# S5 outputs and the norm of k get a place in TensorE's order: a hybrid S5 / DeltaNet / mixture-of-experts layer on one core

## The chip, the cores and the metric

The kernel runs on one NeuronCore of a Trainium2 chip. The time is that of one execution on the device in microseconds (us). Each of the engines TensorE (PE; its weight loads are PEld), VectorE (DVE), ScalarE (ACT), GpSimd (POOL) and SyncE (SP) works through its own list of instructions in order; they wait for each other by semaphores. SP and ScalarE also issue the transfers (DMA); "SPq" and "ACTq" mark such issues.

## The reference, cut to what matters

One layer with 256 latent tokens behind 256 context tokens, width 1024, all in float32.

```python
h  = rmsnorm(x,   norm1) * (1 + sc1)  + sh1        # modulation from silu(c) @ w_mod
hc = rmsnorm(ctx, norm1) * (1 + csc1) + csh1
u, qkv, gate, b, a, br = split(h @ w_in)           # 512, 1536, 512, 8, 8, 2048 columns; the same for hc
qkv = silu(short_conv(qkv))                        # 5 taps along the tokens
# branch A: S5, 32 groups of 16 channels, 64 complex states, two directions
y = d*u + sum over directions of readout(complex_scan(A, B u), C)   # the scan starts from the context's end
ya = z * sigmoid(z @ w_glu + b_glu),  z = gelu(y)
# branch B: gated DeltaNet, 4 heads of 128, chunks of 64, two directions
q = l2norm(q) * 128**-0.5 ;  k = l2norm(k)         # l2norm(t) = t * rsqrt(sum(t*t) + eps)
# per chunk: a triangular solve on k k^T, then a scan over the 8 chunks with a 128 x 128 state
yb = rmsnorm(o) * norm * silu(gate)
ga, gb = sigmoid(br)
x = x + gt1 * ((ga * (ya @ w_branch_a) + gb * (yb @ w_branch_b)) @ w_out)
# mixture of experts: top 4 of 32, w_gate_up 1024 x 2048 and w_down 1024 x 1024 for each, 403 MB in all
out = rmsnorm(x + gt2 * moe(rmsnorm(x, norm2) * (1 + sc2) + sh2), norm_f)
```

## The kernel before

`front` does everything up to DeltaNet's scan over the chunks, `merge` the output projection, `moe` the experts. The experts' weights are streamed once by SP, a tile of 1 MB at a time, into every register that the front part has given back.

The front part is a list of small steps, written out in `ORDER` (line 187) and traced in that order by the loop in `front`. `u`, `k`, `v`, `q`, `gate` and `br` are blocks of 128 columns of the input projection (4, 4, 4, 4, 4 and 16 of them). The first three kinds (`proj_cm`) cover all 512 tokens with 8 matmuls, which the trace shows as 16 instructions `ps<-h,win`. The last three (`proj_lat`) cover the latent tokens only: ScalarE and VectorE split the block's weights into a high and a low half (`wsp`), and TensorE runs 16 instructions `ps<-hx,wsp`. `k`, `v` and `q` go on to the short convolution on VectorE and ScalarE (`conv`: `raw`, `cacc`, `cth`). `mod` is one piece of the modulation of the second half (`ps<-wm,sc`, 1 MB of `w_mod` each). Tiles `win`, `wsp` and `wm` share five buffers of 1 MB.

- `l2k` (line 729, through `l2`, line 693) norms k: ScalarE squares it (`sq`), TensorE sums the squares (`ps<-ones,sq`), VectorE and GpSimd take the root (`rnk`), TensorE spreads it, VectorE multiplies k. `gdn_a` (line 1044) then forms the chunks' matrices, passes them through DRAM (`ad`, `M`) and solves them on VectorE (`fst`, `Y`).
- `s5_in0/1`, `s5_scan` (VectorE) and `s5_steps` (GpSimd, 31 steps on `XL`) are the S5 scan in blocks of 8 tokens.
- `s5_K` (line 490) builds the kernel within a block (`ps<-R,BB` on TensorE, then `KS` on ScalarE and VectorE). `s5_T` (line 558) copies it by 32 transfers of 64 KB into `T`, 16 issued by ScalarE and 16 by SP.
- `s5_out` (line 887) makes S5's output: 64 instructions `ps<-T,U`, then 256 `ps<-R,XL`, then the gelu into `z`.
- `gdn_b0` and `gdn_b1` prepare DeltaNet's scan; they write into registers that `s5_out` reads. `br@3000` are branch-gate blocks with a lower priority, which fill TensorE.

The order of the list is not yet the order on an engine. A planner simulates the program when it is built and lets each engine take, among the instructions whose inputs it believes ready, the one with the best priority; SP alone keeps the written order. A matmul's priority is that of its step (`rank`). `tc.issue_after(ins)` adds an edge to the planner: what the block traces on `ins`'s engine is placed behind `ins` in that engine's order, with no wait for its end. `self.last` is the matmul traced last.

Of the kernel before, what the change touches and what calls it, by code (L numbers as in the profile page):

```python
# [27 lines left out]
class Kern:  # L28
# [114 lines left out]
    def front(self):  # L143
        tc, nc = self.tc, self.nc
        self.smalls()
        self.load_x()
        self.s5_load(0)
        self.mod1()
        self.s5_load(1)
        self.wins, self.winq, self.pair = self.win_order(), [], {}  # L150
        self.ba_load()
        for _ in range(self.WIN0):
            self.win_load()
        self.load_h()
        self.mod1_end()
        self.modulate()
        self.s5_prep()
        self.CC, self.R = [[self.raw[:, i, :16] for i in (2, 3)], None], {}
        self.P = [None, self.s5_P(1)]
        self.P[0] = self.s5_P(0)  # L160
        self.s5_R0()
        self.s5_C()
        step = dict(
            k=self.proj_k(), u=self.proj_u(), v=self.proj_v(), q=self.proj_q(), gate=self.gate(),
            mod=self.mod2(), br=self.br(), ba=self.branch_a())
        for x in self.ORDER.split():
            n, _, times = x.partition("*")
            n, _, pr = n.partition("@")
            for _ in range(int(times or 1)):
                p0 = tc.cur_priority  # L170
                if pr:
                    tc.cur_priority = p0 + int(pr)
                self.rank = tc.cur_priority
                if n in step:
                    next(step[n])()
                else:
                    getattr(self, n)()
                if pr:
                    tc.cur_priority = p0
        self.rank = None  # L180
        assert not any([list(x) for x in step.values()])
        self.gdn_scan()
        tc.cur_priority += 5000
        self.merge()

    ENG_P, ENG_R, ENG_E = "VVVVVGVV", "GGGGGGGG", "VVVV"
    ORDER = """proj_ba u*5 mod*2 gdn_e k mod k s5_in0 s5_in1 mod k mod k s5_scan s5_R1 mod v l2k gdn_a s5_steps
        mod v mod v mod v mod s5_K lat q mod q s5_T mod q mod q mod l2q mod*2 gate*4 br*2 s5_out gdn_b0
        br@3000*14 gdn_b1 s5_glu@500 ba@500*8"""

    def mod1(self):
        nc, I, wk = self.nc, self.I, self.wk
# [386 lines left out]
    def win_order(self):  # L579

        left = {n: iter([c + x // 2 if x % 2 == 0 else None for x in range(b)]) for n, (c, b) in self.W_IN.items()}
        for x in self.ORDER.split():
            n, _, times = x.partition("*")
# [1205 lines left out]
```

## Time and profile before

| | us |
|---|---|
| median of 3 runs (1449.15 to 1454.15) | 1453.27 |
| the profiled execution | 1453.78 |
| its span, first to last instruction | 1452.1 |
| TensorE busy | 1338.0 (92%) |
| VectorE busy | 559.1 (39%) |
| ScalarE busy | 255.4 (18%) |
| GpSimd busy | 179.1 (12%) |

The shares are means over stages with different limits: in the first 200 us VectorE is busy most of the time, from 240 to 470 us TensorE is, and from about 545 us on the transfers run at some 410 to 420 GB/s without a break.

### The profile page before, as it was taken

To read this page: it belongs to the slowest core of one execution; us is meant where nothing else is said; L and a number is where in the kernel's file an instruction comes from. 1 tells how busy PE (TensorE), PEld (TensorE's weight loads), DVE (VectorE), ACT (ScalarE), POOL (GpSimd) and SP (SyncE) were. 2 spreads that over 40 slices of the span, in tenths; PEclk is the share of its full clock that TensorE was granted. 3 is DMA by queue.
4 is the path that set the end of the run, shared out by engine and by line. 5 is a ranking of instruction groups with operands and counts; after the bars stand their busy time and mean duration, and the time that the engine had idled before them with its cause. 6 is when DMAs were issued, how large, how long until landed. Compare 5 with 4: busy or idle time off the path is not lost. (4 is left out here: it accounts for less than half of the span.)

```text
span 1452.1 us, 18531 instructions
## 1 busy us (share of the span) xinstructions
PE 1338.0 (92%) x7469; PEld 600.9 (41%) x7469; DVE 559.1 (39%) x1083; ACT 255.4 (18%) x568; POOL 179.1 (12%) x299
## 2 busy tenths in 40 slices
PE   4799784999999899999999999999999999999985
PEld 1244362768787533333333333333333333333321
DVE  4977977664254403222322322232222222222213
ACT  3224321524301111011110110111011101111001
POOL 1921875111000100000000000000000000000000
PEclk9799896999999899999999999999999999999998
DMA  9464236711638899999999999999999999999994
GB/s 341 193 139 146 88 77 178 223 59 59 197 123 329 281 356 416 419 419 420 419 418 419 420 418 419 419 420 418 419 420 419 418 420 419 419 419 419 419 420 188
DMA packets 93275, 473.06 MB, mean 326 GB/s; under 512 B 24912, under 2 KB 29160, under 8 KB 41344
## 3 DMA queue, kind: packets, MB, share of 16 engines
q1 hardware_dynamic: 73216, 461.08, 79.4%
q10 hardware_dynamic: 19968, 10.73, 3.5%
q8 instruction: 61, 1.00, 0.3%
q14 instruction: 30, 0.25, 0.1%
HBM read 466.52 MB, written 3.16 MB: 323 GB/s over the span
## 5 line engine op out<-in xcount | busy, mean ns | idle before, releaser
L79 PE MATMUL ps<-w,xT 128*64 128x512 f32 x2048 | 485.7, 601 | 9.0 <-DMA w<-in_w_gate_up_dram 8.8
L79 PEld LDWEIGHTS ps<-w,xT 128*64 128x64 f32 x2048 | 137.6, 137 | 272.6 <-issue 241.8
L79 PE MATMUL ps<-w,aT 128*64 128x512 f32 x1024 | 233.1, 597 | 11.4 <-DMA w<-in_w_down_dram 11.1
L1725 DVE SCALAR_TENSOR_TENSOR od<-ps,cs,gt 128x512 f32<-128x512 f32 x31 | 23.3, 750 | 468.7 <-PE ps L79 468.7
L79 PEld LDWEIGHTS ps<-w,aT 128*64 128x64 f32 x1024 | 71.6, 137 | 165.5 <-issue 126.4
L94 DVE TENSOR_TENSOR x<-x,ps 128x512 f32<-128x512 f32 x128 | 84.1, 684 | 66.4 <-PE ps L79 66.4
L1506 POOL CAST selsd<-biad 128x128 fp32r<-128x128 f32 x32 | 9.4, 294 | 703.5 <-PE ps L79 703.5
L97 ACT ACTIVATE odh<-od 128x512 fp32r<-128x512 f32 x31 | 19.5, 629 | 427.0 <-DVE od L1725 427.0
L79 PE MATMUL ps<-h,win 128*128 128x512 f32 x192 | 91.3, 616 | 0.0
L79 PE MATMUL ps<-hx,wsp 128*128 128x256 f32 (+1 forms) x384 | 81.8, 360 | 0.0
L79 PEld LDWEIGHTS ps<-hx,wsp 128*128 128x128 f32 x384 | 62.9, 198 | 20.1 <-issue 9.8
L79 PE MATMUL ps<-h,oh 128*64 128x512 f32 x248 | 63.0, 604 | 0.0
L79 PEld LDWEIGHTS ps<-h,win 128*128 128x128 f32 x192 | 35.0, 195 | 47.6 <-issue 45.8
L97 ACT ACTIVATE sgm<-gt 128x512 f32<-128x512 f32 (+1 forms) x33 | 20.3, 618 | 163.6 <-DVE gt L1696 163.6
L79 PE MATMUL ps<-wm,sc 128*32 128x512 f32 x192 | 29.3, 699 | 20.2 <-DMA wm<-in_w_mod_dram 20.2
L97 ACT ACTIVATE aT<-ps 128x512 f32<-128x512 f32 (+1 forms) x33 | 19.3, 584 | 141.9 <-PE ps L83 141.9
L1696 DVE TENSOR_SCALAR gt<-ps 128x512 f32<-128x512 f32 (+1 forms) x33 | 22.2, 675 | 57.1 <-PE ps L79 57.1
L94 DVE TENSOR_TENSOR wsp<-win,wsp 128x512 fp32r<-128x512 f32 x48 | 32.0, 701 | 23.8 <-ACT wsp L97 23.5
L685 DVE SCALAR_TENSOR_TENSOR cacc<-raw,col_gdn_conv,cacc 128x512 f32<-128x512 f32 (+1 forms) x48 | 36.3, 756 | 5.5 <-ACT cacc L97 5.3
L1506 POOL CAST selsg<-biad 128x256 fp32r<-128x256 f32 x32 | 13.7, 427 | 190.7 <-PE ps L79 184.5
L97 ACT ACTIVATE wsp<-win 128x512 fp32r<-128x512 f32 x48 | 27.5, 624 | 49.2 <-PE ps L79 27.0
L79 PE MATMUL ps<-bias,selsg 128*128 128x512 f32 x64 | 28.6, 472 | 7.1 <-DVE ut L1698 6.6
(367 smaller groups left out, 1465.9 us busy)
## 6 DMA issues: line engine op xcount, KB each, us to landing
w<-in_w_gate_up_dram SPq DMA_DIRECT2D x242, 1024.0 KB
w<-in_w_down_dram SPq DMA_DIRECT2D x121, 1024.0 KB
wm<-in_w_mod_dram SPq DMA_DIRECT2D x24, 1024.0 KB
win<-in_w_in_dram SPq DMA_DIRECT2D x18, 1024.0 KB
w<-in_w_gate_up_dram SPq DMA_DIRECT2D x28, 512.0 KB
w<-in_w_down_dram SPq DMA_DIRECT2D x14, 512.0 KB
wo<-in_w_out_dram SPq DMA_DIRECT2D x4, 1024.0 KB
wa<-in_w_branch_a_dram SPq DMA_DIRECT2D x4, 512.0 KB
```

What stands on the lines that cost most here:

```text
L79: self.last = self.nc.tensor.matmul(out, lhsT, rhs, start=start, stop=stop, **kw)
L94: (eng or self.nc.vector).tensor_tensor(out, a, b, op=op)
L97: self.nc.scalar.activation(out, in_, func, **kw)
L685: nc.vector.scalar_tensor_tensor(acc[:, rows], rt[:, rows, k:k + 64], sc, acc[:, rows], op0=OP.mult, op1=OP.add)
L1506: nc.gpsimd.tensor_copy(v.rearrange("p (n s) -> p n s", s=CAP), dup[:, x:x + n, None].to_broadcast([128, n, CAP]))
L1696: V.tensor_scalar(g, z0, 7.0, None, op0=OP.min)
L1725: V.scalar_tensor_tensor(od, self.pd, self.cs, k.gt2, op0=OP.mult, op1=OP.mult)
```

## The change

`s5_out` and `l2k` are traced inside `issue_after` of the last matmul traced before them. `l2k`, with `gdn_a` and `s5_steps` behind it, moves in the list from behind the first v block to behind the second. One of the fourteen low-priority branch-gate blocks becomes a third normal one, ahead of `s5_out`.

```diff
                 if n in step:
                     next(step[n])()
+                elif n in self.BEHIND:
+
+                    with tc.issue_after(self.last.ins):
+                        getattr(self, n)()
                 else:
                     getattr(self, n)()
...
+    BEHIND = ("l2k", "s5_out")
     ENG_P, ENG_R, ENG_E = "VVVVVGVV", "GGGGGGGG", "VVVV"
-    ORDER = """proj_ba u*5 mod*2 gdn_e k mod k s5_in0 s5_in1 mod k mod k s5_scan s5_R1 mod v l2k gdn_a s5_steps
-        mod v mod v mod v mod s5_K lat q mod q s5_T mod q mod q mod l2q mod*2 gate*4 br*2 s5_out gdn_b0
-        br@3000*14 gdn_b1 s5_glu@500 ba@500*8"""
+    ORDER = """proj_ba u*5 mod*2 gdn_e k mod k s5_in0 s5_in1 mod k mod k s5_scan s5_R1 mod v mod v l2k gdn_a s5_steps
+        mod v mod v mod s5_K lat q mod q s5_T mod q mod q mod l2q mod*2 gate*4 br*3 s5_out gdn_b0
+        br@3000*13 gdn_b1 s5_glu@500 ba@500*8"""
```

## Rows read from the trace of the kernel before

**Rows 1.** Stages: start:end, length, busy us (instructions) by engine, TensorE's clock, DMA share, GB/s.
```profile
145.00:182.00 37.00, 28.81 (x207) 14.36 (x200) 36.73 (x43) 12.16 (x35) 31.97 (x27) 0.86 0.26 86
...
236.00:240.00 4.00, 0.00 (x0) 0.00 (x0) 0.00 (x0) 0.00 (x0) 3.52 (x12) 0.50 0.47 107
...
330.00:400.00 70.00, 69.93 (x661) 57.67 (x660) 25.56 (x48) 29.52 (x70) 4.70 (x5) 0.98 0.43 137
...
545.00:1452.00 907.00, 864.75 (x3933) 302.25 (x3929) 232.24 (x413) 104.71 (x223) 21.51 (x60) 0.99 0.99 410
```

**Rows 2.** TensorE's waits up to 520 us: waiter, awaited, us in total, times, longest.
```profile
PE ps L79 <- DMA T<-KS: 25.0, 3, 15.2
...
PE ps L79 <- ACT sq L97: 8.2, 1, 8.2
```

**Rows 3.** Timeline of TensorE: start, us, instruction, count, idle time before and its end.
```profile
143.73 1.13 PE L79 MATMUL ps<-h,win 128*128 128x512 f32 x2
...
162.32 1.87 PE L79 MATMUL ps<-ones,sq 128*128 128x1 f32 x8 [8.19 <-ACT sq L97]
164.05 2.06 PE L79 MATMUL ps<-h,win 128*128 128x512 f32 x2
```

**Rows 4.** Timeline of ScalarE: v's convolution, then KS.
```profile
161.12 0.63 ACT L97 ACTIVATE cth<-cacc 128x512 f32<-128x512 f32 x1 [14.74 <-DVE cacc L685]
...
207.05 0.60 ACT L97 ACTIVATE KS<-ps 128x512 f32<-128x512 f32 x1 [8.11 <-PE ps L79]
...
208.04 0.55 ACT L97 ACTIVATE KS<-ps 128x448 f32<-128x448 f32 x1 [0.39 <-DVE KS L94]
```

**Rows 5.** Timeline of VectorE around KS.
```profile
199.43 0.21 DVE L94 TENSOR_TENSOR KS<-KS,ps 128x64 f32<-128x64 f32 x1
200.52 1.28 DVE L94 TENSOR_TENSOR A<-A,ps 128x512 f32<-128x512 f32 x2 [0.88 <-PE ps L79]
...
207.68 0.35 DVE L94 TENSOR_TENSOR KS<-KS,dd 128x64 f32<-128x64 f32 x1
208.61 0.22 DVE L94 TENSOR_TENSOR KS<-KS,ps 128x64 f32<-128x64 f32 x1 [0.58 <-ACT KS L97]
```

**Rows 6.** Timeline of SP: its half of the transfers of T.
```profile
208.86 15.93 SPq L564 DMA_DIRECT2D T<-KS  x16
```

**Rows 7.** Timeline of TensorE around q's second and third block.
```profile
210.43 3.07 PE L79 MATMUL ps<-hx,wsp 128*128 128x512 f32 x16
...
240.53 1.03 PE L79 MATMUL ps<-T,U 128*32 128x128 f32 x4 [15.17 <-DMA T<-KS]
241.49 5.40 PE L79 MATMUL ps<-hx,wsp 128*128 128x512 f32 x16
...
247.73 1.07 PE L79 MATMUL ps<-T,U 128*32 128x128 f32 x24
```

**Rows 8.** Timeline of ScalarE: issues of T, then weight splits.
```profile
224.41 16.28 ACTq L564 DMA_DIRECT2D T<-KS  x8
240.74 0.63 ACT L97 ACTIVATE wsp<-win 128x512 fp32r<-128x512 f32 x1 [15.93 <-DMA T<-KS]
...
256.61 0.64 ACT L97 ACTIVATE wsp<-win 128x512 fp32r<-128x512 f32 x1 [1.02 <-PE ps L79]
```

**Rows 9.** Timeline of VectorE: the split for q's third block.
```profile
241.40 0.69 DVE L94 TENSOR_TENSOR wsp<-win,wsp 128x512 fp32r<-128x512 f32 x1 [6.65 <-ACT wsp L97]
```

**Rows 10.** One stage, as rows 1: instructions on XL alone, then on T (PE, PEld).
```profile
241.00:285.00 44.00, 6.21 (x119) 4.51 (x119) 0.00 (x0) 0.00 (x0) 0.00 (x0) 0.94 0.67 203
...
241.00:285.00 44.00, 3.33 (x55) 2.18 (x53) 0.94 0.67 203
```

**Rows 11.** Timeline of TensorE ahead of the first gate.
```profile
254.66 0.88 PE L79 MATMUL ps<-R,XL 64*32 64x128 f32 x18
...
256.47 1.74 PE L79 MATMUL ps<-R,XL 64*32 64x128 f32 x50
```

**Rows 12.** Timeline of GpSimd: the last scan step.
```profile
239.20 0.71 POOL L94 TENSOR_TENSOR XL<-XL,scu 128x64 f32<-128x64 f32 x2
```

**Rows 13.** Waits of SP's queue from 100 to 600 us, as rows 2: weights of the experts.
```profile
SPq L1420 <- PE ps L79: 119.8, 37, 14.5
```

## Prediction

> **What bounds the kernel now.** I read the stages first. From 545 us on the transfers are busy 0.99 of the time and TensorE 864.75 of 907 us, so the mixture of experts is worth nothing to this change except through the moment at which it begins. Between 330 and 400 us TensorE is busy 69.93 of 70 us: whatever TensorE gains or loses before that comes out again behind it. Between 145 and 182 us it is VectorE that is full, 36.73 of 37 us, while TensorE has gaps [rows 1]. The list of TensorE's waits then gives those gaps their names: 25.0 us for the transfers of T out of KS, in three pieces, and 8.2 us in one piece for the squares of k on ScalarE [rows 2]. These two are what the change is aimed at, 33.2 us together. Whether the time behind them goes depends on what the next instruction in TensorE's order would have been waiting for at that moment, so I read the same two stretches on the other engines.
>
> **The norm of k.** TensorE has reached the first sum of squares at 154.1 us and gets its input at 162.32; one matmul of the second v block (two of its sixteen instructions) stands behind it in order [rows 3]. The input is late because ScalarE, in its order, waited 14.74 us for VectorE's convolution of v before it came to the square [rows 4]. With the norm behind the second v block TensorE goes on: that last matmul, the weights of the modulation, the third v block. So 8.2 us of TensorE's time come free, and a little more, since the two v instructions behind the gap took 2.06 us where the same two took 1.13 before it [rows 3]: at most 9.1. Below it is bounded by 0, if the sums of squares again stand in front of something and wait for ScalarE.
>
> What the gain is worth is decided by the next common point, KS. The transfers of T start at 208.86 us [rows 6], right behind the last step of KS on VectorE, which follows two copies on ScalarE (0.60 and 0.55 us); the first of these waited 8.11 us for the matmuls of KS [rows 4]. So TensorE sets KS, and 8.2 us would go through, but VectorE is without a gap until 199.64 (199.43 + 0.21) [rows 5]. From there 0.60 + 0.55 on ScalarE and 0.35 + 0.22 on VectorE give 201.36 as the earliest start of T [rows 4, 5]: 208.86 - 201.36 = 7.5. I take **-7.5**, because the row of KS names TensorE and VectorE is no nearer than that; the bounds are -9.1 and 0.
>
> With the norm two more steps move back by one v block. The 31 scan steps on GpSimd end at 239.92 (239.20 + 0.71) [rows 12], and their first reader, the S5 output, now stands far behind: nothing. The solve of DeltaNet's blocks (with its transfers on ScalarE's queue, which are the same in number) runs on VectorE in the long gap before q's third block, where VectorE sat idle for 6.65 us [rows 9]. A v block is sixteen instructions, 8 x 1.13 = 9.0 us [rows 3]; if the solve moves by all of it, 9.0 - 6.65 = 2.4 us land on the splits of the weights. Bounds 0 and +2.4; I take 0, since KS moves forward while the solve moves back.
>
> **The S5 output, the long wait.** TensorE ends q's second block at 213.50 (210.43 + 3.07), and in the trace the next entries in its order are four instructions on T, three times, the last at 240.53; q's third block starts at 241.49 [rows 7]. The change takes these twelve instructions out. What is next then is q's third block, and it needs weights that ScalarE and VectorE split. ScalarE does that split at 240.74, after 15.93 us idle: it stood there issuing the last eight of its sixteen transfers of T, from 224.41 to 240.69 [rows 8]. These issues keep their place, because the step that makes T stands ahead of q's third block in the written order, and nothing in the change touches that. So TensorE waits until 241.49 as before, with another name in the list of waits. I take **0**; the bounds are 0 and -16.3 (rival B).
>
> The twelve instructions ran in time that was lost anyway. Later they cost 12 x 1.07 / 24 = **+0.5** [rows 7].
>
> Then the rest. From 241 to 285 us the S5 output is spread between the blocks of q, the gates and two branch gates: 6.21 us of the scan part and 3.33 us of the T part [rows 10]. All of it now runs in one piece behind the third branch-gate block, the work being the same. It costs nothing where the next block was ready and was only held up; where the block was not ready, the matmuls covered a wait that is now bare. Bounds 0 and +9.5. The clearest covered wait is ahead of the first gate: two groups of 0.88 and 1.74 us stand there [rows 11], and ScalarE's split for that gate came late, at 256.61, after waiting for TensorE to give a buffer back [rows 8]. I take these two, **+2.6**, because the other blocks show no such wait on ScalarE.
>
> Moving one branch-gate block ahead of the S5 output adds no instruction and no transfer, and the order of the SP queue stays the same, since neither moved step issues anything on it. The steps behind the S5 output get their registers about a block later, while TensorE has thirteen branch-gate blocks to fill with: 0.
>
> **The sum.** -7.5 + 0 + 0.5 + 2.6 = -4.4 us. It is passed on whole: TensorE is full up to 400 us [rows 1], and the loads of the experts' weights wait for TensorE 119.8 us in 37 waits [rows 13], so they start earlier by as much. The profiled execution took 1453.78 us (span 1452.1 and 1.7 around it): 1449.4. The median of the runs is 0.5 lower, so **1449**.
>
> **The rivals.** Case A is this forecast, own range 1443 to 1455.
>
> B: the T wait is really shortened. If the weights of q's third block are split before ScalarE's last eight issues, TensorE can start 0.75 us (241.49 - 240.74) behind 224.41 instead of at 241.49, which is 16.3 us more [rows 7, 8]: 1449 - 16.3 = 1433. For it: the trace names nothing but the issues as what held ScalarE. Against it: the written order puts T first. The Trainium skill (DMA: Bandwidth & Descriptors, "Issuing engines are not separate DMA queues") says that the time a sequencer needs to start a transfer is usually small beside the transfer; by it ScalarE would be through with T at once and this case would be the likeliest. The trace disagrees: eight issues held ScalarE 16.28 us [rows 8].
>
> C: the change does not do what it says; both waits come back under another name, the first as a wait for the sums of squares at their new place. Then -7.5 falls away: 0.5 + 2.6 = +3.1, 1456. For it: VectorE is the full engine there [rows 1], and ScalarE waits for VectorE, not for TensorE.
>
> D, the slower one: the blocks from q's fourth to the third gate lose all their cover. Each waits for a buffer, a load and a split in turn, with nothing between. That is +9.5 instead of +2.6, so -7.5 + 0.5 + 9.5 = +2.5; and a block that follows a gap is slow. q's third block, after the long gap with the granted clock at 0.50, the lower of the two levels, took 5.40 us against 3.07 before it [rows 1, 7], 2.33 more. With four such blocks 2.5 + 9.3 = +11.8: 1465. It is slower by more than 0.5% from three such blocks on. Against it: the transfers and VectorE have room there. The Trainium skill (TensorE: Matmul & The Clock Gate, "HAM oscillation — how this bites in real kernels") describes this very thing, a loop in which TensorE waits for each slice and starts each time at the lower clock; the trace shows it once, behind the long gap.
>
> **How the numbers follow.** A 0.41, B 0.30, C 0.13, D 0.16. What differs by under 0.5% (7.3 us) can't be told from no change, so faster means below 1446 and slower above 1460.5. A quarter of A (0.10) and all of B are faster: 0.40. The rest of A and C are no change: 0.44. D is slower: 0.16. The range of 1431 to 1459 takes in A, C and most of B, and leaves D out.
>
> **What would show it.** Right: no wait of TensorE on the squares of k near 154 us; the first transfer of T some 7 us earlier; the 25 us on T replaced by one wait of 25 to 29 us on the split of weights; the S5 output in one piece of about 10.5 us ahead of DeltaNet's transposes. Wrong: TensorE working between q's second and third block (B); the squares in the list of waits again (C); gaps ahead of each gate with the clock at its lower level (D).

## The result, and the profile after

The changed kernel took 1469.49 us (median of 4 runs, 1462.38 to 1473.44) against 1452.87 before (4 runs, 1449.15 to 1454.15): ratio 1.0113, 95% interval 1.0068 to 1.0158. It is slower by 1.1%, by 16.6 us in the medians and 13.7 in the spans of the two profiled executions (1465.8 against 1452.1). The forecast was 1449, range 1431 to 1459. The mean granted clock of TensorE went from 0.970 to 0.962.

The list of TensorE's waits up to 560 us, answering to [rows 2] (waiter, awaited, us in total, times, longest):

```profile
PE ps L79 <- ACT wsp L97: 27.7, 2, 27.0
...
PE ps L79 <- ACT sq L97: 6.5, 2, 6.2
PE ps L79 <- POOL rnk L94: 6.2, 1, 6.2
```

The 25.0 us on T became 27.0 on the split of weights. The 8.2 us on the squares of k became 6.5 on the same squares, later, and 6.2 on something that was hardly waited for before: the root of the norm, on GpSimd. TensorE's timeline of after shows where, answering to [rows 3, 7]:

```profile
153.09 1.13 PE L79 MATMUL ps<-h,win 128*128 128x512 f32 x2
...
180.35 1.86 PE L79 MATMUL ps<-ones,sq 128*128 128x1 f32 x8 [6.17 <-ACT sq L97]
...
190.67 4.98 PE L79 MATMUL ps<-R,BB 64*32 64x128 f32 x104
201.88 3.78 PE L79 MATMUL ps<-ident,rnk 128*128 128x128 f32 x16 [6.23 <-POOL rnk L94]
...
217.62 2.15 PE L79 MATMUL ps<-R,BB 64*16 64x128 f32 x68
...
221.37 3.04 PE L79 MATMUL ps<-hx,wsp 128*128 128x512 f32 x16
251.39 5.02 PE L79 MATMUL ps<-hx,wsp 128*128 128x512 f32 x16 [26.98 <-ACT wsp L97]
```

At 153.09 TensorE does go on where it used to stand. But the first sum of squares moves from 162.32 to 180.35, 18.0 us, and waits there again. By then all four v blocks are behind it, so its next work would have been KS. The matmuls of KS (R,BB), begun at 187.88 and in earnest at 190.67, are broken off for the root, and end only at 217.62 + 2.15 = 219.77. The root's place on GpSimd is the second half of it. Before, with the step of VectorE that hands the root its input:

```profile
187.23 0.17 DVE L703 TENSOR_SCALAR rnk<-ps 128x16 f32<-128x16 f32 x1
187.48 2.98 POOL L94 TENSOR_TENSOR rnk<-rnk,mhalf 128x16 f32<-128x16 f32 x1 [10.10 <-DVE rnk L703]
190.44 1.17 POOL L94 TENSOR_TENSOR scu<-XL,A 128x64 f32<-128x64 f32 x2
```

And after:

```profile
187.67 1.48 POOL L94 TENSOR_TENSOR scu<-XL,A 128x64 f32<-128x64 f32 x2 [11.41 <-DVE XL L864]
...
198.91 2.91 POOL L94 TENSOR_TENSOR rnk<-rnk,mhalf 128x16 f32<-128x16 f32 x1
```

In after VectorE hands the root its input at 191.18:

```profile
191.18 0.17 DVE L708 TENSOR_SCALAR rnk<-ps 128x16 f32<-128x16 f32 x1
```

By then GpSimd is in the S5 scan, which used to stand behind the root and now stands in front: the root starts at 198.91 although its input is there 7.6 us earlier. Its input is itself 3.9 us later than before (191.35 against 187.40), because the sums are. So the root ends 11.4 us later than before (201.82 against 190.46). From its end to the first transfer of T it is 19.8 us, against 18.4 before. So T starts 12.7 us later, as SP's timeline shows (208.86 in [rows 6]):

```profile
221.59 15.66 SPq L569 DMA_DIRECT2D T<-KS  x16
```

ScalarE, answering to [rows 4, 8], has the squares behind the convolution of the next v block, its copies of KS late, and then the transfers of T ahead of the split as before:

```profile
179.15 0.63 ACT L97 ACTIVATE cth<-cacc 128x512 f32<-128x512 f32 x1 [11.18 <-DVE vT L695]
179.69 0.61 ACT L97 ACTIVATE sq<-kT 128x512 f32<-128x512 f32 x1
...
220.11 1.03 ACT L97 ACTIVATE KS<-ps 128x512 f32<-128x512 f32 x2 [12.40 <-PE ps L79]
235.70 14.97 ACTq L569 DMA_DIRECT2D T<-KS  x9
250.71 1.15 ACT L97 ACTIVATE wsp<-win 128x512 fp32r<-128x512 f32 x2 [14.62 <-DMA T<-KS]
```

By stages (columns as in [rows 1]) VectorE is full up to 182 us as before, and behind it TensorE runs between waits at a granted clock of 0.59, near the lower of its two levels:

```profile
145.00:182.00 37.00, 30.52 (x204) 14.73 (x204) 36.65 (x41) 9.54 (x29) 30.84 (x26) 0.94 0.34 114
...
186.00:206.00 20.00, 13.77 (x152) 10.66 (x155) 11.39 (x25) 3.02 (x5) 17.23 (x33) 0.59 0.01 1
...
330.00:400.00 70.00, 70.00 (x669) 55.38 (x669) 27.46 (x45) 31.11 (x67) 10.64 (x12) 1.00 0.39 140
```

How the loss travels, by landmarks of the two traces: the first transfer of T +12.7, q's third block +9.9 (251.39 against 241.49), the first matmul of w_out +11.6 (below), the span +13.7. TensorE is full from 330 to 400 us, and the lateness is still there behind it.

```profile
461.74 7.03 PE L79 MATMUL ps<-wo,gs 128*128 128x512 f32 x16
```

The same row of before starts at 450.15.

### The profile page after: what moved, and what is told of

Same layout as the page of the kernel before. It is cut to its first block, busy times and chain, and to the rows that moved or that the text cites. A ratio compares the mean times of both kernels' runs of the same rounds, so it can differ in the third digit from the quotient of the medians.

```text
span 1465.8 us, 18529 instructions
## 1 busy us (share of the span) xinstructions
PE 1341.2 (92%) x7469; PEld 606.7 (41%) x7469; DVE 560.5 (38%) x1083; ACT 254.6 (17%) x568; POOL 178.2 (12%) x299
## 5 line engine op out<-in xcount | busy, mean ns | idle before, releaser
L79 PE MATMUL ps<-w,aT 128*64 128x512 f32 x1024 | 233.2, 597 | 11.8 <-DMA w<-in_w_down_dram 11.4
L79 PE MATMUL ps<-hx,wsp 128*128 128x512 f32 (+1 forms) x384 | 78.8, 355 | 29.0 <-ACT wsp L97 27.7
```

The lines of the kernel that those rows point to most:

```text
L79: self.last = self.nc.tensor.matmul(out, lhsT, rhs, start=start, stop=stop, **kw)
```

## The experiments

Ten kernels ran, in three groups, each beside runs of the kernel before on the same chip, whose median was 1452.79 (e1, e2, e4, e5), 1453.34 (e3, e6, e7, e8) and 1453.54 (e9, e10).

**e1, the S5 part alone.** Against the changed kernel:

```diff
-    BEHIND = ("l2k", "s5_out")
+    BEHIND = ("s5_out",)
-    ... mod v mod v l2k gdn_a s5_steps mod v mod v mod s5_K ...
+    ... mod v l2k gdn_a s5_steps mod v mod v mod v mod s5_K ...
```

> Only the S5 half of the change: the S5 output behind q, the gates and three branch-gate blocks, the norm of k where it was. Theory (the norm half costs the time): KS and the first transfer of T as before at about 208.9 us, q's third block at 241.5 +-1.5 us with one wait of about 28 us on the split of weights in place of the 25.0 us on T, and 1453 + 3 = 1456 us, between 1452 and 1460. Rival (the S5 output's matmuls were cover, and without them the blocks wait): 1463 us or more, with waits of TensorE between 241 and 290 us that sum to 8 us or more.

Measured: 1457.36 (10 runs), ratio 1.0034 (1.0014 to 1.0054). The wait on T came back as one wait on the split of weights, with T and the third block slightly earlier than in the kernel before:

```profile
207.40 15.94 SPq L569 DMA_DIRECT2D T<-KS  x16
...
239.80 5.42 PE L79 MATMUL ps<-hx,wsp 128*128 128x512 f32 x16 [27.82 <-ACT wsp L97]
```

Between 241 and 290 us TensorE's waits come to 2.3 us, none over 0.9. So rival D's row of slow, bare blocks isn't there. All 2.3 us stand around the first gate, between 250 and 255 us, where the prediction had looked for lost cover. Third block 1.7 earlier, w_out 2.1 later (452.24): 3.8 us are lost between, where the forecast had 0.5 + 2.6 = 3.1. The S5 part costs a little (4.6 us in the medians) and gains nothing; it isn't the 16 us.

**e2, the norm alone.**

```diff
-    BEHIND = ("l2k", "s5_out")
+    BEHIND = ("l2k",)
-    ... gate*4 br*3 s5_out gdn_b0 br@3000*13 ...
+    ... gate*4 br*2 s5_out gdn_b0 br@3000*14 ...
```

> Only the norm half of the change: the norm of k behind the second v block, the S5 output where it was. Theory: the sums of squares and the root stand in front of KS as in the changed kernel, TensorE waits some 6 us for each, the first transfer of T starts near 221.5 us, the 25 us wait on T is back under its old name, and the time is 1453 + 12 = 1465 us, between 1460 and 1470. Rival (the S5 half costs the time): 1446 to 1453 us, with T starting before 209 us.

Measured: 1461.58 (6 runs), ratio 1.0053 (1.0025 to 1.0082). The two new waits and the late T are all here, without the S5 edge:

```profile
180.16 1.87 PE L79 MATMUL ps<-ones,sq 128*128 128x1 f32 x8 [6.17 <-ACT sq L97]
...
201.68 3.45 PE L79 MATMUL ps<-ident,rnk 128*128 128x128 f32 x16 [6.07 <-POOL rnk L94]
...
220.01 16.43 SPq L569 DMA_DIRECT2D T<-KS  x16
```

The wait on T came back as 13.0 us on T and 8.9 on a load of weights (`win`), not whole under its old name as expected. The norm was forecast at -7.5 and costs time by itself. Its w_out starts at 456.24, 6.1 late; with e1's 2.1 that is 8.2, and after has 11.6. By medians the halves give 4.6 + 8.8 = 13.4 of 16.6; the intervals are too wide to say whether the two parts make each other worse.

**e3, which half of the norm's edit: its place in the written order, or the edge that ties it to TensorE's last matmul.**

```diff
-    BEHIND = ("l2k", "s5_out")
+    BEHIND = ()
-    ... gate*4 br*3 s5_out gdn_b0 br@3000*13 ...
+    ... gate*4 br*2 s5_out gdn_b0 br@3000*14 ...
```

> The norm of k one v block later in the written list, without the edges that place its matmuls behind that block; the S5 output as in the kernel before. Theory (the later place in the list is what moves the norm's pieces in front of KS, the edge itself adds nothing): waits for the squares and the root as in the norm half alone, T from about 220 us on, 1458 to 1464 us. Rival (the edge holds the sums back): the sums run earlier, T starts before 212 us, 1448 to 1455 us.

Measured: 1461.45 (10 runs), ratio 1.0060 (1.0040 to 1.0079), the same waits and the same T as e2:

```profile
PE ps L79 <- ACT sq L97: 6.5, 2, 6.2
PE ps L79 <- POOL rnk L94: 6.0, 1, 6.0
```

The first transfer of T is at 219.76. The edge does nothing to the norm that these runs resolve; the place in the list does it.

**e4, the root put back in front of the scan on GpSimd.** The changed kernel, with

```diff
+                elif n == "s5_steps":
+                    with tc.issue_after(self.powi.ins):
+                        getattr(self, n)()
...
-        self.tt(rn, rn, self.mhalf[:, :4 * nt], OP.pow, self.nc.gpsimd)
+        self.powi = self.nc.gpsimd.tensor_tensor(rn, rn, self.mhalf[:, :4 * nt], op=OP.pow)
```

> The changed kernel, and in addition GpSimd's scan steps are placed behind the root of the norm on GpSimd, as they were in the kernel before. Theory: the wait of 6.2 us for the root falls to under 1 us, KS and the first transfer of T start 6 to 9 us earlier than in the changed kernel (213 to 216 us), and the time is 7 us lower, 1458 to 1464 us; the scan, which now starts later, ends about as it did in the changed kernel. Rival (the root's wait is covered anyway, T is set by ScalarE or VectorE): T near 221.5 us and 1466 to 1472 us.

Measured: 1461.27 (10 runs), ratio 1.0055 (1.0036 to 1.0074). TensorE's wait on the root is gone and T starts 8.9 us earlier than in after:

```profile
190.85 3.36 POOL L712 TENSOR_TENSOR rnk<-rnk,mhalf 128x16 f32<-128x16 f32 x1 [14.86 <-DVE rnk L711]
...
212.65 16.51 SPq L572 DMA_DIRECT2D T<-KS  x16
...
239.35 5.49 PE L79 MATMUL ps<-hx,wsp 128*128 128x512 f32 x16 [24.10 <-ACT wsp L97]
...
273.95 2.05 PE L79 MATMUL ps<-hx,wsp 128*128 128x512 f32 x4 [3.35 <-DVE gx L94]
```

So of the 12.7 us at T, 8.9 are the root's place on GpSimd: 7.6 that it ends earlier, and 1.4 that T follows it sooner. The other 3.8 go with the sums that wait at their new place: the root ends 3.8 us later than before (194.21 against 190.46), and from there T follows after 18.4 us as before. By medians e4 is 8.2 us better than after, though w_out moved only 4.4 (457.32). The third block comes 12.0 us earlier than in after, but the S5 output only 6.0 (287.74 against 293.77). In between TensorE waits 3.35 us for a gate on VectorE, where after has 0.89, and behind that wait the granted clock is 0.78 (272 to 288 us) against 1.00 at the same work in after.

**e5, the norm behind KS.** The changed kernel with the norm not before KS in the order at all:

```diff
-    ... mod v mod v l2k gdn_a s5_steps mod v mod v mod s5_K lat q ...
+    ... mod v mod v mod v mod v mod s5_K l2k gdn_a s5_steps lat q ...
```

> The changed kernel with the norm of k moved further back, behind the step that makes KS (and behind its last matmul on TensorE), so that nothing of the norm stands in front of KS. Theory: the matmuls of KS run from about 181 us on without a wait, the first transfer of T starts between 197 and 205 us, q's third block some 16 to 24 us earlier than in the changed kernel's 251.4 us, and the time is 1440 to 1452 us unless the solve, now later, is met by the scan of DeltaNet. Rival (the norm's place in front of KS does not matter): T no earlier than 218 us and 1465 us or more.

Measured: 1452.22 (10 runs), ratio 0.9980 (0.9961 to 0.9999).

```profile
201.16 22.01 SPq L568 DMA_DIRECT2D T<-KS  x16
...
214.76 5.76 PE L79 MATMUL ps<-ident,rnk 128*128 128x128 f32 x32 [11.00 <-POOL rnk L94]
```

T starts at 201.16. The prediction had worked out 201.36 as the earliest that VectorE allows [rows 5], and that step is borne out once the norm is out of KS's way. The time fell 17.3 us below after, to the kernel before's, a little above the 1440 to 1452 expected. But e5 holds the S5 part too. Beside e1, which has only that, T is 6.2 us earlier and the time 5.1 us shorter, by intervals that don't overlap. So a norm out of KS's way gains 5.1 of the 7.5 us that the prediction had for it. Left behind KS is a wait of 11.0 us on the root, and four waits on splits of weights make 12.9; which of them keeps the rest isn't shown.

**e6, rival B: is it ScalarE's issues that hold q's third block?** e1 with all 32 transfers of T issued by SP:

```diff
-                (nc.scalar, nc.sync)[j % 2].dma_start(
+                nc.sync.dma_start(
```

> The S5 half alone, and all 32 transfers of T issued by SP, so that ScalarE issues none of them. Theory (what holds q's third block is ScalarE, standing at its issues of T): the wait of 27.8 us on the split goes, q's third block starts by 222 us and the fourth follows; the loads behind T on SP's queue come some 15 us later, so part of it is paid back at the gates, and the time is 4 to 12 us under the S5 half alone, 1445 to 1453 us. Rival (the split waits for a buffer or for T's own traffic): q's third block near 240 us as before and 1456 us or more.

Measured: 1456.20 (10 runs), ratio 1.0016 (0.9998 to 1.0034).

```profile
225.77 2.07 PE L79 MATMUL ps<-hx,wsp 128*128 128x512 f32 x4 [12.17 <-ACT wsp L97]
...
237.79 0.81 DVE L94 TENSOR_TENSOR wsp<-win,wsp 128x512 fp32r<-128x512 f32 x1
...
238.65 3.78 PE L79 MATMUL ps<-hx,wsp 128*128 128x256 f32 x12 [10.81 <-DVE wsp L94]
```

The third block began 14.0 us earlier than in e1, so the issues did hold ScalarE; but after four matmuls it stood 10.8 us for VectorE's half of the same split. VectorE had been in the steps of DeltaNet's solve (`fst`, `Y`) from 225.86 on and came to the split at 237.79, with no gap before it. And SP itself was held:

```profile
209.00 25.81 SPq L569 DMA_DIRECT2D T<-KS  x32
234.86 0.71 SPq L221 DMA_DIRECT2D wm<-in_w_mod_dram  x1
```

The next load of weights left SP only at 234.86. The expected 1445 to 1453 was missed: 14 us at the block became about 1 us at the end, which the intervals of e1 and e6 can't tell from none, with w_out at 455.84, later than e1's 452.24. Freeing one engine isn't enough there.

**e7, the producer moved instead of the reader.** e1 with the step that makes T behind q in the list:

```diff
-    ... lat q mod q s5_T mod q mod q mod l2q ...
+    ... lat q mod q mod q mod q s5_T mod l2q ...
```

> The S5 half alone, with the step that makes T moved in the list from behind q's second block to behind q's fourth, so that on ScalarE and on SP the third and fourth block of q and the first gates' load stand in front of T's transfers. Theory: q's third and fourth block run without the long wait, which shrinks from 28 to under 12 us in sum (ahead of the gates), and the time is 1438 to 1449 us. Rival (the wait moves to the first gate whole, because ScalarE's issues last as long there): waits on splits of 20 us or more in sum, 1453 us or more.

Measured: 1444.42 (5 runs), ratio 0.9929 (0.9903 to 0.9955), 12.9 us under e1; w_out starts at 439.30. No long wait on a split is left: q's third and fourth block run from 214.13 on. ScalarE's first issue of T is at 208.62, about where it was (207.40 in e1). What changed is that the splits now pass between its issues, no more than two of which stand together, and that SP starts its half at 214.32 instead of 207.40. The largest new wait is the squares of q, behind q's convolution, whose steps alternate with the issues of T on ScalarE:

```profile
208.62 0.79 ACTq L569 DMA_DIRECT2D T<-KS  x1
...
212.09 1.14 ACT L97 ACTIVATE wsp<-win 128x512 fp32r<-128x512 f32 x2
...
214.13 5.87 PE L79 MATMUL ps<-hx,wsp 128*128 128x512 f32 x32
...
236.98 3.65 PE L79 MATMUL ps<-ones,sq 128*128 128x1 f32 x16 [11.92 <-ACT sq L97]
```

**e8, both repairs together: e5 with T behind q.**

```diff
-    ... s5_K l2k gdn_a s5_steps lat q mod q s5_T mod q mod q mod l2q ...
+    ... s5_K l2k gdn_a s5_steps lat q mod q mod q mod q s5_T mod l2q ...
```

> The changed kernel with both moves: the norm of k behind the step that makes KS, and T behind q's fourth block. Theory: the gains of the two add in part, no wait of TensorE over 12 us between 150 and 290 us, 1436 to 1447 us. Rival (the norm of k, now later, comes between q's blocks and the solve on VectorE stands in the way of the splits): 1450 us or more.

Measured: 1435.55 (4 runs), ratio 0.9865 (0.9825 to 0.9905): the best here, just under the 1436 to 1447 expected, 17.8 us under the kernel before and 33.9 under the changed one. q's third block starts at 203.92, its fourth at 209.21, and the largest wait left in the stretch is the root, at 220.79:

```profile
209.21 1.21 PE L79 MATMUL ps<-hx,wsp 128*128 128x512 f32 x4 [1.33 <-ACT wsp L97]
...
220.79 6.07 PE L79 MATMUL ps<-ident,rnk 128*128 128x128 f32 x32 [7.31 <-POOL rnk L94]
```

**e9, is the S5 edge worth anything in e8?**

```diff
-    BEHIND = ("l2k", "s5_out")
+    BEHIND = ("l2k",)
```

> The best kernel so far (norm of k behind the step that makes KS, T behind q's fourth block) without the edge that places the S5 output: the planner may spread it again between the blocks of q and the gates. Theory (with T out of the way the S5 output's matmuls are cover, as in the stretch from 241 us of the kernel before): 1 to 4 us less than with the edge, 1431 to 1436 us. Rival (the planner again puts T's readers in front of blocks that are ready, and they wait for T): waits on T of 8 us or more, 1440 us or more.

Measured: 1438.85 (4 runs), ratio 0.9901 (0.9876 to 0.9927). The longest wait on T is 0.57 us, so neither the 1431 to 1436 us expected nor the rival's long waits came. Against e8's interval this can't be told from no difference: with T behind q the S5 output has nothing long to wait for, wherever it stands.

**e10, e8 with the root first on GpSimd,** by the edit of e4:

> The best kernel so far, and GpSimd's scan steps placed behind the root of the norm. Theory (TensorE's wait for the root, 7.3 us, is on the path): the wait falls under 2 us and the time by 4 to 7 us, 1428 to 1432 us. Rival (the scan's 50 us on GpSimd now start so late that the S5 output waits for them): a wait for the scan ahead of the S5 output and 1436 us or more.

Measured: 1440.14 (4 runs), ratio 0.9924 (0.9896 to 0.9953).

```profile
214.62 2.05 PE L79 MATMUL ps<-ident,rnk 128*128 128x128 f32 x16 [0.65 <-POOL rnk L711]
...
269.68 9.09 PE L79 MATMUL ps<-R,XL 64*32 64x128 f32 x256 [2.34 <-POOL XL L94]
```

The 7.3 us on the root went down to 0.65, and the 4 to 7 us expected from it didn't come. The scan, now later, holds the S5 output 2.3 us, as the rival had it. VectorE's steps on k are waited for 2.6 us in all, and a load of the modulation's weights 2.2, where e8 has no such waits. That is 7.1 us for the 6.7 gained, and the intervals of e8 and e10 overlap.

## Why the prediction was wrong, step by step

**The norm of k, -7.5: wrong, and the whole miss.** The step that failed is "With the norm behind the second v block TensorE goes on [...] 8.2 us of TensorE's time come free", and "8.2 us would go through". The first half holds (153.09 in the timeline of after). The second doesn't, for two reasons that the trace of before holds. First, it was never asked when the squares would be ready at the new place; the only price put on a move by one v block, for the solve, was TensorE's 9.0 us. But ScalarE reaches the squares only behind VectorE's convolution, and VectorE was full [rows 1]: one block later in the list was 18.0 us later there (161.12 in [rows 4] to 179.15), and so were the first sums (162.32 to 180.35). The sums therefore waited again, at a place now next to KS. With the root's place put right (e4) +3.8 at T are left for that. Second, the root on GpSimd was not followed at all. I costed the scan's move ("nothing", by its reader) and didn't ask what the scan would now stand in front of. e4 prices that at +8.9. Together T is at +12.7 where the step had -7.5.

I had written the bound "0, if the sums of squares again stand in front of something and wait for ScalarE". That names the mechanism but leaves out a loss: the new place stood in front of KS, so the wait there could hold KS back. Rival C said the wait would come back and priced it at 1456; it was right in kind, and its price assumed the same length and no follower on GpSimd.

**The solve, 0: right, though not for the reason given.** KS didn't move forward. The solve moved back 12.8 us with it (its first `fst` from 216.63 to 229.42), and VectorE still stood idle before the split, 3.62 us against 6.65 [rows 9]:

```profile
251.37 0.69 DVE L94 TENSOR_TENSOR wsp<-win,wsp 128x512 fp32r<-128x512 f32 x1 [3.62 <-ACT wsp L97]
```

**The long wait on T, 0: right.** One wait of 27.0 us on the split of weights, 25 to 29 forecast. **Rival B's 16.3 us:** e6 shows that its premise, the issues holding ScalarE, is real, and that freeing ScalarE alone doesn't bring the gain. e7 brings about its condition, the splits ahead of the last issues, and 12.9 of the 16.3 us came. The Trainium skill's sentence weighed there (DMA: Bandwidth & Descriptors, "Issuing engines are not separate DMA queues") says that starting a transfer usually takes little time beside the transfer; in after too, nine issues held ScalarE 14.97 us. How long one transfer of T takes no row here shows, so the comparison itself is not tested.

**Lost cover and later T instructions, +3.1: right in size.** e1 has 3.8 in its one profile. The S5 output does run in one piece from 293.77 us on, 8.07 us on XL and 2.37 on T, 10.4 where 10.5 was forecast:

```profile
293.77 1.97 PE L79 MATMUL ps<-T,U 128*32 128x128 f32 x62
296.36 5.24 PE L79 MATMUL ps<-R,XL 64*32 64x128 f32 x181
302.82 2.40 PE L79 MATMUL ps<-R,XL 64*32 64x128 f32 x73 [1.22 <-issue]
```

**Rival D, 1465:** its time is nearest to the result, its place isn't the cause. Between 252 and 500 us no wait of TensorE in after is over 1.3 us; the granted clock is 0.95 on the mean from 251 to 294 us, and the 0.59 stands earlier, at 186 to 206 us, around the wait on the root. That a block behind a gap is slow, rival D's own premise, the trace of before shows twice and not once: also behind the 8.2 us wait, 2.06 us against 1.13 [rows 3].

**Passing on whole: right in kind.** 11.6 at w_out and 13.7 in the span; the last 2.1 us, and the 2.9 between spans and medians, are within what runs of after differ by (11 us), and aren't explained.

## What to carry to other kernels

A step moved back in one engine's order takes its instructions on every engine with it: for each, ask what it will now stand behind and what it will stand in front of, and price the move in the time of the engine that is full in that stretch, not of the one that waits (here 18.0 us, not 9.0). A wait taken out of TensorE's order ends only if the next instruction's inputs are ready; here they came from the engine that was issuing the transfers, so moving the reader renamed 25 us, while moving the producer in the list gave 13 us (e7 beside e1) and 17 (e8 beside e5). A bound of zero needs a reason that excludes a loss; "it may wait again" is not one when the new place stands in front of the critical step.

## What the hardware showed that was not expected

An issue of a transfer of T had no fixed price: 16.28 / 8 = 2.0 us on ScalarE before [rows 8], 14.97 / 9 = 1.7 in after, 25.81 / 32 = 0.8 on SP alone in e6, and 3.41 / 4 = 0.9 on ScalarE in e8, where other work of ScalarE stands between them:

```profile
209.29 3.41 ACTq L568 DMA_DIRECT2D T<-KS  x4
212.74 0.42 ACT L97 ACTIVATE cth<-cacc 128x256 f32<-128x256 f32 x1 [3.07 <-DMA T<-KS]
```

What sets it wasn't tried. And the waits of the norm cost more than their length: the sixteen transposes behind the root took 3.78 us in after and 2.05 in e10, at the same form: the granted clock was 0.50 there (201.9 to 205.7 us) and 1.00 in e10 (214 to 217 us).
